# A token-major V stage, a shorter candidate list and other gather rates in a one-core hybrid decoder step

## The chip, the cores and the metric

The kernel runs on one core of one Trainium2 chip (trn2). The metric is the device time of one execution in microseconds. Three timed runs of the kernel before and one profiled execution are at hand.

## The reference, cut to what matters

The program computes one layer of a decoder for a prompt (16 meta tokens and 512 tokens) and 8 samples of 8 tokens: token mixers, then a product-key expert layer ("PEER"), then a final RMSNorm. The expert layer and the final norm are what the change touches:

```python
qh = einsum('td,de->te', xb, w_query)                  # 8 heads x 2 halves x 128
s  = einsum('thpd,hpnd->thpn', qh, sub_keys)           # 128 keys per half
sv, si = top_k(s, 16)                                  # best 16 keys of each half
cand = sv[:, :, 0, :, None] + sv[:, :, 1, None, :]     # 16 x 16 sums per head
top_s, pos = top_k(cand, 16)                           # best 16 pairs -> expert 128*i + j
gate = softmax(top_s)
act  = gelu(einsum('thkd,td->thk', expert_u[eidx], xb))
y    = einsum('thk,thkd->td', gate * act, expert_v[eidx])
h = h + y;  out = rms_norm(h, norm_final)              # 576 tokens of 1024
```

There are 16,384 experts, each a row of 1,024 numbers in `peer_u` and one in `peer_v`.

## The kernel before

All arithmetic is in fp32. A product is three fp32r matmuls (`mm3`, lines 135 to 139): each operand is split into a high part (written by ScalarE) and a low part (what is left, written by VectorE), and high times high, high times low and low times high are summed in PSUM.

Of the 576 tokens the first 384 (`ND`) are handled densely and the last 192 (`NG`) by gathers. **Dense** means that the hidden value of every expert is computed for every token. The experts are taken 128 at a time, a "half"; two halves make a pair, and there are 64 pairs (`NP`) and so 128 halves in the **U stage** (`hidden`, from line 1439) and as many in the **V stage** (`experts`, from line 1528). In the U stage a half's weights (128 x 1024) come by DMA seven halves ahead (`fetch`), ScalarE writes their high part three halves ahead (`hi`, line 1432), VectorE their low part two ahead (`lo`, line 1438), and 24 matmuls of 384 columns give the hidden values, which ScalarE passes through Gelu (line 1471) and which go to DRAM for the first 48 pairs (`gz`). In the V stage `prepare` reads them back, VectorE multiplies by the gates `wj` (line 1516), ScalarE and VectorE split the product into `ah` and `al` (lines 1518, 1523), and the 24 matmuls of a half have the weights' 128 x 128 pieces as the stationary operand and 384 columns of `ah` or `al` as the moving one, so that eight PSUM banks `py[d]` hold the output with its features on the partitions.

The **gates** come from the selection. `select` forms candidate sums of a head's best 16 and 16 keys, finds the best 16 of them with `top16` (`max`, `max_index`, `match_replace` on VectorE), and turns ranks back into key numbers. `taken`, `spread`, `onehots`, `scaled`, `scatter` and `stored` turn them, for the dense tokens, into a gate for every expert in DRAM (`wd`). `select(0)` belongs to the first block of gathered tokens and runs within `scored`, beside the scores of the other tokens; the other four blocks' selections are interleaved with the U stage by `route`.

The **gathered** tokens' experts come by indirect DMA, 128 rows of 4 KB at a time, 192 times from `peer_u` and 192 times from `peer_v` (`NROW` is 384; `gather_begin` on GpSimd's queue, `gather` on VectorE at lines 1344 and 1351). How many per half is a planner's matter: `gcred` grows by `GQ0` in each of the U stage's first 96 halves, by `GQ1` in its last 32, by `GQ2` in the V stage's first 32, and then by `rate`, which is worked out so that all are done `GTAIL` pairs before the end. `fill` spends VectorE's time of a half (`HALF` less `WL` and `MUL`) on gathers first and then on the steps of `route`; the numbers after `yield` are its costs in us. From `hidden` on, the order of PE, VectorE, ScalarE and SP is fixed as the program emits it (`in_order`). GpSimd's isn't, and what stands before `hidden` is ordered by the scheduler.

At the end of `experts` the last pair's matmuls run by `d`; VectorE adds the residual, ScalarE squares, PE sums over the partitions, the root is broadcast by PE, and eight transfers of 192 KB go out on SP's and ScalarE's queues (line 1598). The gathered tokens' own norm and output are `gather_out`.

Of the kernel before, what the change touches and what calls it, by code (L numbers as in the profile page):

```python
# [22 lines left out]
P = 128  # L23
# [7 lines left out]
H = 4  # L31
# [25 lines left out]
NCAND = 8 * TOPK + 8  # L57
# [9 lines left out]
GQ0, GQ1, GQ2, GTAIL = 1.25, 2.1, 1.65, 6  # L67
# [53 lines left out]
class Net:  # L121
# [108 lines left out]
    def build(self):  # L230
        tc, nc, I, O = self.tc, self.nc, self.I, self.O
        self.right = ExitStack()
        with self.pool("const") as cp, self.pool("wraw", 3) as self.wraw, self.pool("whl", 2) as self.whl, \
# [5 lines left out]
            self.yd = self.dp.tile([P, KC, ND], F32, name="yd")  # L239
# [5 lines left out]
            with self.pool("y") as yp:  # L245
# [688 lines left out]
    def merge(self):  # L934
# [3 lines left out]
        with self.pool("mg") as mp, self.pool("mw", 2) as wp, \  # L938
# [34 lines left out]
            for k in range(KC):  # L973
                nc.sync.dma_start(self.yd[:, k, :], self.y[k][:, :ND])
# [11 lines left out]
    def ffn_sink(self, o, w, ps, wp):  # L986
# [5 lines left out]
        def sink(k, t):  # L992
# [36 lines left out]
    def scored(self):  # L1029
# [4 lines left out]
        self.blks = [(NT - P, P), (ND, NX)] + TBLK  # L1034
# [13 lines left out]
        self.ijg = rp.tile([P, 3, ND], F16, name="ijg")  # L1048
        self.glo = rp.tile([P, ND], F32, name="glo")
# [3 lines left out]
        with self.pool("keys", 1, side="right") as kp, self.pool("qw", 2, side="right") as wp:  # L1053
            keys = kp.tile([P, 2 * PH, NK], F32, name="keys")
            nc.sync.dma_start(keys, I["keys"])
            for o, w in SEG:
# [52 lines left out]
                if o + w == NT:  # L1109
# [4 lines left out]
                    for d, v in ((self.x2h, self.xg[0]), (self.x2l, self.xg[1])):  # L1114
                        for k in range(KC):
                            nc.sync.dma_start(d[k][:, o:].bitcast(F32), v[k][:, :ND - o].bitcast(F32))

    def select(self, b):

# [24 lines left out]
        nc.vector.tensor_scalar(au[:n], ti[:n], 4, None, op0=ALU.logical_shift_right)  # L1144
        nc.vector.tensor_scalar(bu[:n], ti[:n], 15, None, op0=ALU.bitwise_and)
# [3 lines left out]
        nc.vector.scalar_tensor_tensor(t[:n], a[:n], 8.0, r[:n], op0=ALU.is_ge, op1=ALU.mult)  # L1149
        nc.vector.tensor_add(a[:n], a[:n], t[:n])  # L1150
        nc.vector.tensor_sub(r[:n], r[:n], t[:n])
        yield 0.9 + f
        out = []
        for x, rank in enumerate((a, r)):
            sb = small(f"sb{x}")
            nc.vector.tensor_copy(sb[:n], si[:n, b, :H, x, :])
# [19 lines left out]
        nc.vector.tensor_tensor(g[:n], g[:n], sm[:n, :, None].to_broadcast([n, H, TOPK]), op=ALU.mult)  # L1176
# [22 lines left out]
    def taken(self, b):  # L1199
# [12 lines left out]
        yield 1.3  # L1212
# [474 lines left out]
```

## Time and profile before

| | us |
|---|---|
| median of 3 runs | 1967.29 (1966.35 to 1970.87) |
| profiled execution, its own time | 1970.01 |
| its span in the profile | 1968.2 |
| PE busy | 1895.1 (96%) |
| VectorE busy | 1609.1 (82%) |
| ScalarE busy | 912.8 (46%) |
| GpSimd busy | 741.8 (38%) |
| mean granted TensorE clock | 0.982 of full speed |
| DMA, mean over the span | 279 GB/s |

The span runs from the first to the last instruction of the profiled execution; the time beside it is that execution's own. Matmul ends are modelled and matmuls overlap, so a busy PE says only that it had no gap.

### The profile page before, as it was taken

What the parts mean: (1) busy time and instruction counts of PE and PEld (TensorE: products, weight loads), DVE (VectorE), ACT (ScalarE), POOL (GpSimd) and SP (SyncE); (2) the same over time, 40 slices, a digit from 0 to 9 for tenths busy, and PEclk for the clock granted to TensorE, in tenths of its full rate; (3) what the DMA queues carried; (4) which work ended last, traced back from release to release, by engine and by line L of the source; (5) the groups of instructions that cost most, each with busy time, mean ns of one, the idle gap of its engine ahead of it and who ended that gap; (6) DMA issues with size and microseconds to landing.
All of it is one profiled execution on the core that took longest, in us unless ns stands there. A gap on an engine that the chain in (4) does not pass through costs nothing.

```text
span 1968.2 us, 33353 instructions
## 1 busy us (share of the span) xinstructions
PE 1895.1 (96%) x12481; PEld 1829.2 (93%) x12481; DVE 1609.1 (82%) x3016; ACT 912.8 (46%) x1594; POOL 741.8 (38%) x537
## 2 busy tenths in 40 slices
PE   8999999999999998999999999999999999999997
PEld 6898999788999997999999999999999999999996
DVE  6676676686366689999999998688999879889895
ACT  5542334263225454445777999533333323333332
POOL 1110010310001366243343444466776556656530
PEclk9998999999999998999999999999999999999998
DMA  7344233466455635799898999999999999999991
GB/s 264 111 152 140 92 104 103 149 184 197 159 164 164 200 125 168 265 328 325 340 358 322 394 396 368 384 390 395 400 400 400 399 401 400 399 402 400 401 340 57
DMA packets 219904, 548.20 MB, mean 279 GB/s; under 512 B 31332, under 2 KB 96612, under 8 KB 218076
## 3 DMA queue, kind: packets, MB, share of 16 engines
q1 hardware_dynamic: 163724, 343.90, 49.4%
q0 software_dynamic: 55296, 201.35, 26.5%
q8 instruction: 98, 1.61, 0.3%
q10 hardware_dynamic: 720, 0.80, 0.1%
q14 instruction: 66, 0.54, 0.1%
HBM read 474.89 MB, written 69.77 MB: 277 GB/s over the span
## 4 chain that ended last, share of the span: by engine, by line
PE 35%; DMA 19%; DVE 5%; issue 1%; POOL 0%; ACT 0%; SPq 0%; POOLq 0%; DVEq 0%; ACTq 0%
DMA wr<-in_v 9%; PE pz L137 8%; PE pz L139 8%; PE pz L138 8%; DMA wj<-wd 8%; PE py L138 2%; PE py L139 2%; PE py L137 2%; PE pw L1262 2%; DMA gz<-gz 2%; DVE ul L1438 1%; DVE gr L1344 1%; DMA yr<-yd 1%; DVE yt L1351 1%; DVE al L1523 0%
## 5 line engine op out<-in xcount | busy, mean ns | idle before, releaser
L1332 POOL DMA_INDIRECT gr<-in_ur,gi x192 | 308.5, 1607 | 272.9 <-DVE yt L1351 193.3
L1432 ACT ACTIVATE uh<-wr 128x1024 fp32r<-128x1024 f32 x256 | 270.5, 1057 | 250.2 <-PE py L138 123.8
L1332 POOL DMA_INDIRECT gr<-in_v,gi x192 | 289.4, 1507 | 238.0 <-DVE gr L1344 175.7
L138 PE MATMUL py<-al,uh 128*128 128x384 f32 x1024 | 349.2, 341 | 17.4 <-DVE al L1523 17.1
L137 PE MATMUL py<-ah,uh 128*128 128x384 f32 x1024 | 347.7, 340 | 4.0 <-ACT ah L1518 3.4
L137 PE MATMUL pz<-x2h,uh 128*128 128x384 f32 x1024 | 347.6, 339 | 0.0
L139 PE MATMUL py<-ah,ul 128*128 128x384 f32 x1024 | 347.5, 339 | 0.0
L139 PE MATMUL pz<-x2h,ul 128*128 128x384 f32 x1024 | 343.6, 336 | 2.0 <-DVE ul L1438 2.0
L138 PE MATMUL pz<-x2l,uh 128*128 128x384 f32 x1024 | 343.4, 335 | 0.0
L1438 DVE TENSOR_TENSOR ul<-wr,uh 128x1024 fp32r<-128x1024 f32 x256 | 311.9, 1218 | 15.6 <-issue 6.8
L1351 DVE SCALAR_TENSOR_TENSOR yt<-gr,ga,yt 128x1024 f32<-128x1024 f32 x192 | 245.8, 1280 | 15.0 <-DMA gr<-in_v,gi 12.5
L137 PE MATMUL acc<-xnh,wh 128*128 128x296 f32 (+1 forms) x768 | 233.7, 305 | 8.0 <-ACT xnh L296 6.3
L1344 DVE SCALAR_TENSOR_TENSOR gr<-gr,xt 128x1024 f32<-128x1024 f32 x192 | 233.5, 1217 | 6.4 <-DMA gr<-in_ur,gi 6.2
L139 PE MATMUL acc<-xnh,wl 128*128 128x296 f32 (+1 forms) x768 | 234.5, 306 | 0.5 <-DVE wl L133 0.5
L138 PE MATMUL acc<-xnl,wh 128*128 128x296 f32 (+1 forms) x768 | 233.9, 305 | 0.5 <-DVE xnl L297 0.5
L132 ACT ACTIVATE wh<-wr 128x1024 fp32r<-128x1024 f32 x104 | 110.0, 1059 | 226.7 <-PE acc L138 71.9
L138 PEld LDWEIGHTS py<-al,uh 128*128 128x128 f32 x1024 | 194.5, 190 | 21.3 <-DVE al L1523 21.2
L137 PEld LDWEIGHTS py<-ah,uh 128*128 128x128 f32 x1024 | 194.3, 190 | 5.3 <-ACT ah L1518 4.3
L139 PEld LDWEIGHTS pz<-x2h,ul 128*128 128x128 f32 x1024 | 193.0, 188 | 2.7 <-DVE ul L1438 2.6
L139 PEld LDWEIGHTS py<-ah,ul 128*128 128x128 f32 x1024 | 194.4, 190 | 0.0
L138 PEld LDWEIGHTS pz<-x2l,uh 128*128 128x128 f32 x1024 | 193.3, 189 | 0.0
L137 PEld LDWEIGHTS pz<-x2h,uh 128*128 128x128 f32 x1024 | 193.1, 189 | 0.1
(427 smaller groups left out, 3436.7 us busy)
## 6 DMA issues: line engine op xcount, KB each, us to landing
wr<-in_u SPq DMA_DIRECT2D x128, 512.0 KB
wr<-in_v SPq DMA_DIRECT2D x128, 512.0 KB
gz<-gz SPq DMA_DIRECT2D x96, 384.0 KB
wr<-in_w_in SPq DMA_DIRECT2D x48, 512.0 KB
wd<-wst SPq DMA_DIRECT2D x12, 2048.0 KB
wj<-wd SPq DMA_DIRECT2D x96, 256.0 KB
wr<-in_w_q SPq DMA_DIRECT2D x32, 512.0 KB
wr<-in_w_out SPq DMA_DIRECT2D x16, 512.0 KB
```

Of the source, the lines that this page charges most:

```text
L132: self.last_hi = self.nc.scalar.activation(hi, src, AF.Copy)
L137: mm(out, wh, xh, start=start, stop=False)
L138: mm(out, wh, xl, start=False, stop=False)
L139: self.last_mm = mm(out, wl, xh, start=False, stop=stop)
L1262: nc.tensor.matmul(pw[:, u, :], oh[0][:, t], oh[2 + x][:, t], start=x == 0, stop=x == 1)
L1332: nc.gpsimd.indirect_dma_start(out=t, out_offset=None, in_=src, in_offset=bass.IndirectOffsetOnAxis(ap=self.gi[z][:, x, c:c + 1], axis=0))
L1344: nc.vector.scalar_tensor_tensor(t, t, 1.0, xt, op0=ALU.mult, op1=ALU.mult, accum_out=ga[:, c:c + 1])
L1351: nc.vector.scalar_tensor_tensor(yt, t, ga[:, c:c + 1], yt, op0=ALU.mult, op1=ALU.add)
L1432: self.nc.scalar.activation(w, self.raws[s], AF.Copy)
L1438: self.nc.vector.tensor_sub(w, self.raws.pop(s), self.ws[s][0].bitcast(F32))
```

## The change

The V stage is turned round: the stationary operand is now 128 tokens of `ah` or `al`, the moving one 512 columns of the weights, so a half is 18 matmuls of 512 columns, and six PSUM banks hold the output with its tokens on the partitions. All products of a half with the weights' high part and `ah` come first, then the low part with `ah`, then the high part with `al`. The residual is added by PE: 24 fp32 matmuls with an identity, three in each of eight halves. The last pair runs by block of 128 tokens, and each block is normed over its free axis and sent out on its own. The first block's output goes in transfers of 112 and 15 rows, by two column halves; its first token goes out alone through the old feature-major output. The new `ND` is 1 and `NG` 575 for the host's outputs; `MD` is the old 384.

The candidate sums are 80 for each head (16 + 7 x 8 + 8) instead of 136, with three more small steps to turn a position into ranks. The two key-number copies become one, the last step of each sum tree writes the result itself, the gate's scaling moves into `select`, the copies of `taken` go to ScalarE, and two of the comparisons of `onehots` become one of twice the size. `GQ0` is 1.32 instead of 1.25, `GTAIL` 4 instead of 6. The other changes of the diff are the new names.

```diff
-NG = P + NX
-ND = NT - NG
+MG = P + NX
+MD = NT - MG
+ND, NG = 1, NT - 1
-NCAND = 8 * TOPK + 8
+NCAND = TOPK + 7 * 8 + 8
-GQ0, GQ1, GQ2, GTAIL = 1.25, 2.1, 1.65, 6
+GQ0, GQ1, GQ2, GTAIL = 1.32, 2.1, 1.65, 4
...
     def select(self, b):
-        nc.vector.tensor_tensor(cd[:n, :, :P].rearrange("p h (a b) -> p h a b", a=8),
-                                s0[:, :, :8, None].to_broadcast([n, H, 8, TOPK]),
-                                s1[:, :, None, :].to_broadcast([n, H, 8, TOPK]), op=ALU.add)
-        nc.vector.tensor_tensor(cd[:n, :, P:], s0[:, :, 8:], s1[:, :, 0:1].to_broadcast([n, H, 8]), op=ALU.add)
-        yield 0.2 + 1.15 * f
+        nc.vector.tensor_tensor(cd[:n, :, :TOPK], s0[:, :, 0:1].to_broadcast([n, H, TOPK]), s1, op=ALU.add)
+        nc.vector.tensor_tensor(cd[:n, :, TOPK:-8].rearrange("p h (a b) -> p h a b", b=8),
+                                s0[:, :, 1:8, None].to_broadcast([n, H, 7, 8]),
+                                s1[:, :, None, :8].to_broadcast([n, H, 7, 8]), op=ALU.add)
+        nc.vector.tensor_tensor(cd[:n, :, -8:], s0[:, :, 8:], s1[:, :, 0:1].to_broadcast([n, H, 8]), op=ALU.add)
+        yield 0.4 + 0.7 * f
...
-            yield 2.4
+            yield 1.93
...
+        w = small("rw")
+        nc.vector.tensor_scalar(w[:n], a[:n], 1.0, 8.0, op0=ALU.is_equal, op1=ALU.mult)
+        nc.vector.tensor_add(r[:n], r[:n], w[:n])
+        nc.vector.tensor_scalar(a[:n], a[:n], -1.0, 0.0, op0=ALU.add, op1=ALU.max)
...
+        sbs = wp.tile([P, H, 2, TOPK], BF, name="sb", tag="sb")
+        nc.vector.tensor_copy(sbs[:n], si[:n, b, :H])
...
-            v = small(f"ix{x}")
-            nc.vector.tensor_copy(v[:n], e[:n, :, 0, :])
...
     def taken(self, b):
-            nc.vector.tensor_copy(self.ijg[:, x, sl], p[:, :n])
-        gs = self.wp.tile([P, P], F32, name="gs", tag="gs")
-        nc.vector.tensor_scalar(gs[:, :n], g[:, :n], GSC, None, op0=ALU.mult)
-        nc.vector.tensor_copy(self.ijg[:, 2, sl], gs[:, :n])
-        nc.vector.tensor_sub(self.glo[:, sl], gs[:, :n], self.ijg[:, 2, sl])
+            nc.scalar.activation(self.ijg[:, x, sl], p[:, :n], AF.Copy)
+        nc.vector.tensor_copy(self.ijg[:, 2, sl], g[:, :n])
+        nc.vector.tensor_sub(self.glo[:, sl], g[:, :n], self.ijg[:, 2, sl])
...
     def onehots(self, q, last):
-        nc.vector.tensor_tensor(oh[1], io, rb(1), op=ALU.is_equal)
-        yield 0.61
-        nc.vector.tensor_tensor(oh[0], io, rb(0), op=ALU.is_equal)
-        yield 0.61
+        nc.vector.tensor_tensor(ij, io, r[:, :2].rearrange("p x t e -> p (x t) e")[:, :, None, :].to_broadcast([P, 2 * TG, N8, E8]),
+                                op=ALU.is_equal)
+        yield 1.15
...
     def experts(self):
+            def products(b, a, w, start=False, stop=False):
+
+                for c in range(2):
+                    nc.tensor.matmul(py[b][:, c, :], a[:, b * P:(b + 1) * P], w[:, 4 * c:4 * c + 4, :], start=start, stop=stop)
...
-                        for d in range(KC):
-                            self.mm3(py[d][:, :ND], wh[:, d, :], wl[:, d, :], ah[:, h], al[:, h], self.half == NK, False)
+                        for b in range(nb):
+                            products(b, ah[:, h], wh, start=s == NK)
+                        for b in range(nb):
+                            products(b, ah[:, h], wl)
+                        for b in range(nb):
+                            products(b, al[:, h], wh)
+                    d = s - NK - KEEP - 8
+                    if 0 <= d < KC:
+
+                        for b in range(nb):
+                            nc.tensor.matmul(py[b][:, d // 4, d % 4 * P:(d % 4 + 1) * P], self.y[d][:, b * P:(b + 1) * P], self.c("ident"),
+                                             start=False, stop=False)
...
+            for b in range(nb):
                 for h in range(2):
...
+                    wh, wl = self.ws[last - 1 + h]
+                    products(b, ah[:, h], wh)
+                    products(b, ah[:, h], wl)
+                    products(b, al[:, h], wh, stop=h == 1)
+                o = wp.tile([P, D], F32, name="yo", tag="yo", bufs=nb)
+                v = wp.tile([P, 1], F32, name="yv", tag="yv", bufs=nb)
+                nc.scalar.activation(o, py[b].rearrange("p a b -> p (a b)"), AF.Square, accum_out=v)
+                nc.vector.tensor_scalar(v, v, 1.0 / D, EPS, op0=ALU.mult, op1=ALU.add)
+                self.rsqrt(v, wp, bufs=2)
+                for c in range(2):
+                    sl = slice(c * 512, (c + 1) * 512)
+                    nc.vector.scalar_tensor_tensor(o[:, sl], py[b][:, c, :], v, self.gf[:, sl], op0=ALU.mult, op1=ALU.mult)
+                    if b:
+                        (nc.scalar if c else nc.sync).dma_start(self.O["yg"][b * P - ND:(b + 1) * P - ND, sl], o[:, sl])
+                    else:
+
+                        for n0, n1 in ((16, P), (ND, 16)):
+                            nc.sync.dma_start(self.O["yg"][n0 - ND:n1 - ND, sl], o[n0:n1, sl])
+                if b == 0:
+                    first = o
+
             for k in range(KC):
...
+                nc.tensor.matmul(one[:, k:k + 1], first[:ND, k * P:(k + 1) * P], self.c("ones")[:1, :1], start=True, stop=True,
+                                 skip_group_check=True)
+            v = wp.tile([P, KC], F32, name="y1")
+            nc.scalar.activation(v, one, AF.Copy)
+            nc.sync.dma_start(self.O["y"].rearrange("p k a -> p (k a)"), v)
```

## Rows read from the trace of the kernel before

**Rows 1.** The page, the span in 40 slices: DMA rate in GB/s.

```profile
GB/s 264 111 152 140 92 104 103 149 184 197 159 164 164 200 125 168 265 328 325 340 358 322 394 396 368 384 390 395 400 400 400 399 401 400 399 402 400 401 340 57
```

**Rows 2.** Windows by stage: length, busy us per engine, clock, DMA share, GB/s.

```profile
918.00:1250.00 332.00, 331.96 (x2416) 323.89 (x2415) 309.20 (x509) 279.53 (x670) 136.28 (x89) 1.00 0.94 361
1384.00:1517.50 133.50, 133.38 (x768) 133.12 (x769) 132.57 (x151) 46.54 (x50) 96.38 (x56) 1.00 1.03 400
1517.50:1900.20 382.70, 362.03 (x2017) 357.29 (x2016) 337.92 (x380) 124.70 (x130) 230.89 (x139) 0.98 1.03 400
1900.20:1942.10 41.90, 41.90 (x244) 41.90 (x243) 29.61 (x41) 15.14 (x17) 0.00 (x0) 1.00 0.43 142
```

**Rows 3.** The page, the chain that ended last, by line.

```profile
DMA wr<-in_v 9%; PE pz L137 8%; PE pz L139 8%; PE pz L138 8%; DMA wj<-wd 8%; PE py L138 2%; PE py L139 2%; PE py L137 2%; PE pw L1262 2%; DMA gz<-gz 2%; DVE ul L1438 1%; DVE gr L1344 1%; DMA yr<-yd 1%; DVE yt L1351 1%; DVE al L1523 0%
```

**Rows 4.** The page, costliest groups: busy us, mean ns, idle before.

```profile
L138 PE MATMUL py<-al,uh 128*128 128x384 f32 x1024 | 349.2, 341 | 17.4 <-DVE al L1523 17.1
L1351 DVE SCALAR_TENSOR_TENSOR yt<-gr,ga,yt 128x1024 f32<-128x1024 f32 x192 | 245.8, 1280 | 15.0 <-DMA gr<-in_v,gi 12.5
```

**Rows 5.** Windows of line 1332 alone, the indirect gathers issued on GpSimd.

```profile
1384.00:1517.50 133.50, 96.38 (x56) 1.00 1.03 400
1517.50:1900.20 382.70, 230.89 (x139) 0.98 1.03 400
```

**Rows 6.** PE's timeline (start us, us): matmuls of 256 and 384 columns.

```profile
764.93 0.28 PE L1091 MATMUL pq<-x2h,wh 128*128 128x256 f32 x1
...
767.32 0.28 PE L1091 MATMUL pq<-x2h,wh 128*128 128x256 f32 x1
...
1919.69 0.34 PE L137 MATMUL py<-ah,uh 128*128 128x384 f32 x1
...
1934.77 0.34 PE L137 MATMUL py<-ah,uh 128*128 128x384 f32 x1
```

**Rows 7.** The chain in order of time: four plain fp32 matmuls of 128 columns.

```profile
782.87 0.44 PE psc L1067 x4
```

**Rows 8.** Groups by form: search and fp32 matmul, ScalarE and VectorE on long rows.

```profile
L1021 DVE FIND_INDEX8 si<-sv,sc 128x8 uint32<-128x128 f32 x64 | 18.1, 282 | 0.0
L1021 DVE FIND_INDEX8 ti<-tv,cand 128x8 uint32<-128x136 f32 x36 | 10.1, 292 | 0.0
L772 PE MATMUL pss<-vm,ke 64*128 64x512 f32 x16 | 7.9, 615 | 1.4 <-DVE vm L764 1.4
L307 ACT ACTIVATE xt<-xt 128x1024 f32<-128x1024 f32 x4 | 4.2, 1060 | 1.6 <-DMA xt<-in_x 1.5
L794 DVE SCALAR_TENSOR_TENSOR at<-pkq,decay 128x512 f32<-128x512 f32 x4 | 2.7, 687 | 0.0
```

**Rows 9.** Timeline around the end of `select(0)`: VectorE, GpSimd (twice), PE.

```profile
765.57 0.47 DVE L1181 SCALAR_TENSOR_TENSOR gi<-ix,ix 128x128 int32<-128x128 bf16 x2
...
766.12 1.15 POOL L1332 DMA_INDIRECT gr<-in_ur,gi  x1 [2.98 <-DVE gi L1181]
...
771.03 4.68 POOL L133 TENSOR_TENSOR wl<-wr,wh 128x1024 fp32r<-128x1024 f32 x2
...
773.43 2.08 PE L1094 MATMUL pq<-x2h,wl 128*128 128x256 f32 x8 [5.72 <-POOL wl L133]
```

**Rows 10.** Timeline of the end: PE, VectorE (two), SP's queue.

```profile
1950.20 0.34 PE L139 MATMUL py<-ah,ul 128*128 128x384 f32 x1
...
1953.18 0.16 DVE L214 TENSOR_SCALAR rmsr<-py 128x3 f32<-128x3 f32 x1 [1.59 <-PE py L1586]
...
1954.42 0.16 DVE L163 TENSOR_TENSOR rmsr<-rsq,rst 128x3 f32<-128x3 f32 x1
...
1957.49 4.53 SPq L1598 DMA_DIRECT2D out_y<-yo  x4
```

**Rows 11.** Window after the last transfer's data: as in rows 2.

```profile
1964.00:1965.00 1.00, 0.00 (x0) 0.00 (x0) 0.00 (x0) 0.00 (x0) 0.00 (x0) 0.50 0.00 0
```

More of the change, by code (lines that the diff above doesn't have):

```diff
@@ L250, in build @@
                 with self.pool("x2") as xp:
-                    self.x2h = [xp.tile([P, ND], F32R, name=f"x2h{k}") for k in range(KC)]
-                    self.x2l = [xp.tile([P, ND], F32R, name=f"x2l{k}") for k in range(KC)]
+                    self.x2h = [xp.tile([P, MD], F32R, name=f"x2h{k}") for k in range(KC)]
+                    self.x2l = [xp.tile([P, MD], F32R, name=f"x2l{k}") for k in range(KC)]
                     with self.pool("x2g") as gp:
@@ L997, in sink @@
                 self.split(self.xg[0][k], self.xg[1][k], t)
-                for x, (dst, v, a) in enumerate(((self.xt, t, w - NG), (self.yt, self.y[k], ND))):
+                for x, (dst, v, a) in enumerate(((self.xt, t, w - MG), (self.yt, self.y[k], MD))):
                     if k % 2 == 0:
@@ L1165, in select @@
             w = TOPK
+            v = small(f"ix{x}")
             while w > 1:
                 w //= 2
-                nc.vector.tensor_add(e[:n, :, :w, :], e[:n, :, :w, :], e[:n, :, w:2 * w, :])
-                yield (w * H * TOPK) * 0.53e-3 + 0.1
-            v = small(f"ix{x}")
-            nc.vector.tensor_copy(v[:n], e[:n, :, 0, :])
+                nc.vector.tensor_add(e[:n, :, :w, :] if w > 1 else v[:n, :, None, :], e[:n, :, :w, :], e[:n, :, w:2 * w, :])
+                yield (w * H * TOPK) * 0.53e-3 + 0.15
             out.append(v.rearrange("p h k -> p (h k)"))
@@ L1443, in hidden @@
         tc, nc, I = self.tc, self.nc, self.I
-        self.wd = self.dp.tile([ND // TB, P, NK, TB], F32, name="wd")
-        self.gz = [self.dp.tile([P, 2, ND], F32, name=f"gz{j}") for j in range(NP - KEEP // 2)]
+        self.wd = self.dp.tile([MD // TB, P, NK, TB], F32, name="wd")
+        self.gz = [self.dp.tile([P, 2, MD], F32, name=f"gz{j}") for j in range(NP - KEEP // 2)]
         self.gdone, self.gcred, self.gready = 0, 0.0, True
@@ L1532, in experts @@
         self.run_due()
+        nb, last = MD // P, 2 * NK - 1
         with ExitStack() as es:
             yps = es.enter_context(self.pool("ey", 1, space=PSUM))
-            py = [yps.tile([P, 512], F32, name=f"py{d}") for d in range(KC)]
-            py = py[4:] + py[:4]
+            one = yps.tile([P, 2, 512], F32, name="one")[:, 0, :KC]
+            py = [yps.tile([P, 2, 512], F32, name=f"py{b}") for b in range(nb)]
+            py = py[1:] + py[:1]
             rate = (NROW - self.gdone - KEEP * GQ2) / (2 * (NP - GTAIL) - KEEP)
+            def products(b, a, w, start=False, stop=False):
+                for c in range(2):
+                    nc.tensor.matmul(py[b][:, c, :], a[:, b * P:(b + 1) * P], w[:, 4 * c:4 * c + 4, :], start=start, stop=stop)
             for k in range(NP, 2 * NP):
@@ L1556, in experts @@
                         self.gready, self.routing = False, self.gather_out()
-                    self.lo(self.half + 2)
-                    self.gates(self.half - NK + JG + 3)
+                    self.lo(s + 2)
+                    self.gates(s - NK + JG + 3)
                 if k == NP + KEEP // 2 - 1:
@@ L1562, in experts @@
                     self.gf = wp.tile([P, D], F32, name="gf")
-                    self.y = [wp.tile([P, ND], F32, name=f"yr{k}") for k in range(KC)]
+                    self.y = [wp.tile([P, MD], F32, name=f"yr{k}") for k in range(KC)]
                     nc.sync.dma_start(self.gf, I["gain"].to_broadcast([P, D]))
@@ L1568, in experts @@
                 pass
-            nb = (ND + P - 1) // P
-            sq = [wp.tile([P, ND], F32, name="rmssum" if d == 0 else "rmssq", tag="rmssum" if d == 0 else "rmssq", bufs=1 if d == 0 else 3)
-                  for d in range(KC)]
-            for d in range(KC):
+            for b in range(nb):
                 for h in range(2):
-                    w = self.ws[2 * NK - 2 + h]
-                    self.mm3(py[d][:, :ND], w[0][:, d, :], w[1][:, d, :], ah[:, h], al[:, h], False, h == 1)
-                nc.vector.tensor_add(self.y[d], self.y[d], py[d][:, :ND])
-                if 1 < d:
-                    nc.vector.tensor_add(sq[0], sq[0], sq[d - 1])
-                nc.scalar.activation(sq[d], self.y[d], AF.Square)
@@ L1582, in experts @@
-            col, t = py[0][:, :nb], py[1][:, :ND]
-            w = [min(P, ND - b * P) for b in range(nb)]
-            for b in range(nb):
-                for x in (0, KC - 1):
-                    nc.tensor.matmul(col[:w[b], b:b + 1], sq[x][:, b * P:b * P + w[b]], self.c("ones")[:, :1], start=x == 0, stop=x > 0)
-            rs = self.rms_cols(col, t, w, wp)
-            rb = wp.tile([P, ND], F32, name="rb")
-            nc.scalar.activation(rb, rs, AF.Copy)
-            for k in range(KC):
-                g = self.p("norm_final")[:, k:k + 1]
-                o = wp.tile([P, ND], F32, name="yo", bufs=KC)
-                if k in (2, 6):
-                    nc.scalar.activation(o, self.y[k], AF.Copy, scale=g)
-                    nc.gpsimd.tensor_mul(o, o, rb)
-                else:
-                    nc.vector.scalar_tensor_tensor(o, self.y[k], g, rs, op0=ALU.mult, op1=ALU.mult)
-                (nc.scalar if k % 2 else nc.sync).dma_start(self.O["y"][:, k, :], o)
+                    wh, wl = self.ws[last - 1 + h]
```

71 lines of the change are left out of this document (35 added, 36 removed).

## The prediction

> **What bounds the kernel now.** I read the slices first, then the windows by stage, the chain and the waits. The slices show DMA near 400 GB/s from slice 29 to slice 38 and below that nearly everywhere else [rows 1]. The windows say what limits each stage. In the middle of the U stage PE is busy 331.96 of 332 us and DMA runs at 361 GB/s: PE sets the pace. In the V stage's first 32 halves (133.5 us, 4.17 us a half) PE, VectorE (132.57) and DMA (400 GB/s) are all full. From there to the last gather, 382.7 us, DMA stays at 400 GB/s while PE idles 20.7 us and VectorE 44.8: DMA sets the pace. In the 41.9 us after it PE is full and DMA falls to 142 GB/s [rows 2]. The chain agrees: transfers of weights and gates hold the most of it beside the U stage's matmuls [rows 3]. PE's one large V wait, 17.1 us for `al` [rows 4], sits inside that DMA-bound stretch, so it is a symptom: taking it away lets PE reach the next late transfer sooner and no more.
>
> **What DMA has to move.** The planner's credits give 96 x 1.25 + 32 x 2.1 = 187 gathers in the U stage, 32 x 1.65 = 53 in the V stage's first 32 halves, and 144 in the next 84 halves (116 = 2 x 58 less 32). The trace has 56 and 139 issues there, with the rest a few issues ahead [rows 5]. A gather is 128 x 4 KB, 0.524 MB. A half also needs 0.524 MB of weights, 0.197 of `gz` and 0.197 of `wj` by the tiles' shapes. For 84 halves that is 77.1 MB, with 144 gathers 152.6 MB; 400 GB/s over 382.7 us is 153.1 MB [rows 2]. So the stretch is its bytes at 400 GB/s.
>
> **The gather rates.** `GQ0` at 1.32 moves 96 x 0.07 = 6.7 gathers, 3.5 MB, into the U stage. `GTAIL` at 4 lets the rest end at half 120, not 116, so four halves that ran at PE's pace with an idle DMA now share the load: their weights and `gz`, 4 x 0.721 = 2.9 MB, fall inside the stretch. It must move 153.1 - 3.5 + 2.9 = 152.5 MB, 381.2 us at 400 GB/s, and reaches half 120. Six halves are left before the last pair, where ten were. Their price is PE's.
>
> **PE's price of a half.** From start to start, 20 matmuls of 256 columns take 2.39 us, 119.5 ns each, and 87 of 384 columns 15.08 us, 173.3 ns each [rows 6]. The line through both gives 227.2 ns at 512: 18 of them are 4.09 us against 24 x 173.3 = 4.16. No row has an fp32r matmul of 512 columns, nor one with token data as the stationary operand. The bounds are 213 ns (columns at 2.4 GHz, nothing added) and 440: four plain fp32 matmuls of 128 columns take 0.44 us [rows 7], and 512 columns at that rate as much; one of 512 lasts 615 ns from its start to its end [rows 8]. I take 227, since it is the same kind of matmul.
>
> The Trainium skill (TensorE: Matmul & The Clock Gate, Back-to-back issue gap) gives columns / 2.4 + 2.5 ns, 162.5 at 384; the row shows 173.3, so it doesn't hold for this form here. By it a half would be 3.88 us and my sum 1.6 us less.
>
> Ten halves at 4.19 were 41.9 us [rows 2]; six at 4.09 are 24.5. From half 32 to the last pair: 382.7 + 41.9 = 424.6 before, 381.2 + 24.5 = 405.7 now, **-18.9 us**. Bounds: only the moved bytes, -8.8; or PE alone, 94 x 4.09 + 3.6 = 388.1, -36.5. The 3.6 is the identity matmuls: 24 x 0.11 = 2.6 [rows 7], and 1 us that I put on for changing between the two kinds. They come in halves 40 to 47, at 4.33 us a half by DMA, where PE then needs 4.54; the lag of 8 x 0.21 = 1.7 us at most is made up from the 0.24 us a half that PE has over in the 73 that follow, so nothing is added. They wait for `yr`, and the whole PE queue stands behind them, but those loads are issued eight halves, some 34 us, ahead. In the first 32 halves PE would give 32 x 0.07 = 2.2 us, but VectorE and DMA are as full; I take 0, with 2.2 as the other end.
>
> **The U stage.** 6.7 more gathers cost VectorE 6.7 x 1.28 = 8.6 us [rows 4] and DMA 3.5 MB over some 440 us, 8 GB/s on 361. VectorE is free for 22.8 us in the middle window [rows 2], and it gets back about 2.8 us for each of 3.5 selections (next part), the merged comparisons and `taken`. So nothing is added, and since PE is full nothing is won. The copies of `taken` wait on ScalarE for PE's transposes, with the next `hi` behind them; `hi` runs three halves ahead. If the cover were gone: +8.6.
>
> **The front.** PE waits 5.72 us for a low part from GpSimd, which stands behind four gathers, which wait for `select(0)`'s last step [rows 9]. A search over 128 columns takes 282 ns, over 136 292 [rows 8]: 10 ns for 8 columns, 70 for the 56 that go, and `select(0)` has 8 heads x 5 searches, 2.8 us. The shorter sums and the copies that go pay for the three new steps within some 0.3 us. GpSimd was free for 2.98 us before its first gather, so it can start as much earlier: **-2.8 us**. Bounds: 0, if the scheduler puts something else there, and -5.7, if the gap closes.
>
> **The end.** The last pair is 36 x 0.227 = 8.17 us after 48 x 0.173 = 8.32: **-0.15**. From PE's last matmul, 1950.20 + 0.34, to the end of the span are 17.7 us [rows 10]. Now each block needs a square (1.06 us, rows 8 has the like from SBUF), the root's small steps (1953.18 to 1954.58, 1.40 us, rows 10) and two products of 512 columns (0.69 each, rows 8): 3.8 us, after 2.7 us of PE. With T as PE's end, block 0 is done at T - 1.6 and block 1, whose small steps stand behind it on VectorE, at T + 1.2. Block 1's second transfer is issued by ScalarE and waits there for that product, and block 2's square stands behind it: T + 1.5 to T + 2.6. Its products end at T + 5.3, the copy of the first token and its transfer on SP at T + 6.2. The old last issue ended at 1962.02, 6.2 us before the span's end [rows 10]; so T + 12.4, **-5.3 us**. Bounds: -8 (no queueing on ScalarE, and with the data gone before 1964 [rows 11] only some 4.7 us after the last issue), and -3.
>
> **The sum.** -18.9 - 2.8 - 0.15 - 5.3 = -27.2. The profiled execution took 1970.0 us, its span 1968.2 with 1.8 around it; it becomes 1942.8. The runs' median is 2.7 below the profiled execution, so the median is forecast at 1940.
>
> **Rivals.** (a) *The later end of the gathers buys nothing.* After the last gather come `gather_out`'s steps, and with six halves instead of ten they, or the DMA's prefetch of the last weights, could hold the last pair; then only the 3.5 MB count, 8.8 us, and the time is 1950. For it: those steps have 17 us less; against it: 24.5 us are left, and VectorE was free for 12.3 of the 41.9 us [rows 2]. (b) *The U stage can't take the gathers*, VectorE becomes the bound there, +8.6: 1949. For it: its windows are nearly full; against: the 22.8 us. (c) *400 GB/s is not a ceiling but what was asked for*, and the V stage runs at PE's 388.1 us: 1923. Against it, PE idled 20.7 us at that rate and ten slices lie at 399 to 402 [rows 1]. The Trainium skill (DMA: Bandwidth & Descriptors, Specifications) has a fabric ceiling of 435 GB/s, and the trace stays under it. (d) *Slower: the wide fp32r matmul doesn't hold the line.* Nothing is felt up to 4.33 / 18 = 241 ns, as DMA hides it; all that is won is lost at (405.7 + 27.2) / 94 / 18 = 256 ns, and 260 ns give 1974 and more. For it: no such row; against: one line through both widths, and the weight loads get longer cover. That the change doesn't do what it says I hold for excluded where it counts bytes and columns.
>
> **Chances and range.** Forecast (1934 to 1946) 0.62; (a) 0.14; (b) 0.10; (c) 0.06; (d) 0.05, of which 0.04 is slower than before; the rest spread between. A difference under 0.2% (4 us) can't be told from none here. Faster 0.94, same 0.02, slower 0.04. The range takes in (a) and (b) and the bounds of front and end: 1929 to 1953.
>
> **What would show it.** Right: V windows at 400 GB/s to half 120, about 7 fewer gathers left when the V stage starts, matmuls 227 ns apart, a gap before the scores' low part of some 3 us, about 12 us from PE's last product to the end. Wrong: PE full in the V stage's later part, or waits of PE in the U stage, or matmuls above 241 ns.

## The result, and the profile after

The changed kernel takes 1940.03 us (median of 4 runs, 1938.06 to 1944.29); the kernel before, run beside it, 1966.82 (1966.28 to 1970.87). The ratio is 0.9862, 95% interval 0.984 to 0.9885: 26.8 us faster, as forecast (1940, -27.2). The steps behind that number did not all hold. The profiled execution took 1941.62 us, span 1939.4.

The page's slices answer to [rows 1]:

```profile
GB/s 267 103 158 156 87 112 100 140 190 181 175 166 149 211 130 158 248 343 332 348 354 344 398 396 380 376 401 397 402 400 401 397 399 402 400 398 401 399 401 103
```

The windows by stage answer to [rows 2], same columns: the middle of the U stage, V's first 32 halves, from there to the last gather, and from there to the last pair:

```profile
914.40:1246.40 332.00, 331.92 (x2404) 323.94 (x2403) 307.33 (x449) 278.39 (x669) 151.15 (x94) 1.00 0.97 368
...
1377.30:1511.90 134.60, 134.60 (x577) 108.31 (x578) 132.02 (x153) 46.49 (x50) 93.09 (x56) 1.00 1.04 401
1511.90:1897.70 385.80, 380.18 (x1648) 304.35 (x1647) 337.20 (x376) 129.65 (x137) 222.47 (x133) 1.00 1.03 397
1897.70:1921.10 23.40, 22.13 (x95) 17.54 (x94) 20.96 (x33) 8.09 (x10) 0.00 (x0) 1.00 0.23 75
```

DMA is at 397 to 401 GB/s there, as before. What has changed is the end: 23.4 us after the last gather instead of 41.9. 133 gathers are issued in the long stretch where there were 139 [rows 5]. PE, idle for 20.7 us there before, is idle for 5.6. The chain of waits in order of time (start, us, what), pieces of the V stage:

```profile
1377.29 172.46 PE py L1546 x738
1549.76 0.67 PE py L1564 x6
1550.42 4.20 PE py L1546 x18
...
1584.49 120.41 PE py L1546 x516
...
1709.20 7.90 DMA wr<-in_v
...
1875.09 15.87 DMA wj<-wd
```

By this chain PE sets the pace up to 1705 us; from 1709 to 1891 us transfers make up some 150 of the 182 us. A product of 512 columns takes 172.46 / 738 = 233.7 ns and a half 4.20 us, more than the old form's 4.16. The eight identity steps take 0.67 us each. PE's V groups on the page no longer wait for `al` (17.1 us in [rows 4]); 4.8 us are left for `ul` and 2.0 for `ah`:

```profile
L1546 PE MATMUL py<-ul,ah 128*128 128x512 f32 x768 | 201.3, 396 | 4.8 <-DVE ul L1440 4.8
L1546 PE MATMUL py<-uh,ah 128*128 128x512 f32 x768 | 201.6, 396 | 2.6 <-ACT ah L1520 2.0
```

The bytes of the long stretch, from the DMA view of 1511.9 to 1897.7 us (its rate in 40 slices, and the total):

```profile
GB/s 394 388 401 399 399 402 402 395 400 402 401 400 399 404 395 400 402 403 398 399 403 389 397 400 406 397 401 401 403 396 401 403 392 399 402 404 398 400 402 292
DMA packets 56956, 153.09 MB, mean 397 GB/s; under 512 B 5433, under 2 KB 22657, under 8 KB 56934
```

Profile against profile, in us:

| part | before | after | forecast | measured |
|---|---|---|---|---|
| start to the first scores' product (`pq`) | 653.0 | 649.1 | 0 | -3.9 |
| front, to the first `pz<-x2l` | 145.0 | 145.3 | -2.8 | +0.3 |
| U stage, to the first V product | 586.0 | 582.9 | 0 | -3.1 |
| V, first 32 halves | 133.5 | 134.6 | 0 | +1.1 |
| V, to the last gather | 382.7 | 385.8 | -1.5 | +3.1 |
| V, to the last pair | 41.9 | 23.4 | -17.4 | -18.5 |
| last pair | 8.4 | 8.6 | -0.15 | +0.2 |
| PE's end to the end of the span | 17.7 | 9.7 | -5.3 | -8.0 |

The first line is no gain. Up to that point both profiles have the same 4604 matmuls in the same order and 796 VectorE instructions, and the twelve kernels below, which are the same there, have their first `pq` between 645.9 and 655.6. From 130 to 260 us the granted clock was 0.93 in the profile before and in the latest of the twelve, 0.99 in the changed kernel's and in the earliest. The windows of 130 to 260 us, before and then after (the last three numbers are the clock, the DMA share and GB/s):

```profile
130.00:260.00 130.00, 126.52 (x941) 118.74 (x940) 91.09 (x152) 43.84 (x69) 9.48 (x27) 0.93 0.40 120
```

```profile
130.00:260.00 130.00, 125.72 (x979) 118.70 (x978) 96.69 (x168) 48.82 (x75) 9.49 (x27) 0.99 0.47 127
```

A median has this scatter in it too, so the experiments are read by stage.

### The profile page after: what moved, and what is told of

It is laid out like the page before. It is cut to its first block, busy times and chain, and to the rows that moved or that the text cites. A ratio compares the mean times of both kernels' runs of the same rounds, so it can differ in the third digit from the quotient of the medians.

```text
span 1939.4 us, 31893 instructions
## 1 busy us (share of the span) xinstructions
PE 1889.3 (97%) x11759; PEld 1722.4 (89%) x11759; DVE 1592.7 (82%) x2962; ACT 909.2 (47%) x1598; POOL 745.1 (38%) x535
## 4 chain that ended last, share of the span: by engine, by line
PE 78%; DMA 11%; DVE 9%; issue 1%; ACT 1%; SPq 0%; DVEq 0%; ACTq 0%
PE py L1546 18%; PE pz L138 9%; PE pz L140 9%; PE pz L139 9%; PE acc L138 4%; PE acc L140 4%; PE acc L139 4%; DMA wr<-in_v 4%; DMA wj<-wd 3%; PE pw L1264 2%; PE py L664 1%; PE pz L659 1%; PE pq L1095 1%; PE pq L1092 1%; PE pbr L138 1%
## 5 line engine op out<-in xcount | busy, mean ns | idle before, releaser
L1334 POOL DMA_INDIRECT gr<-in_ur,gi x192 | 302.8, 1577 | 265.1 <-DVE yt L1353 200.7
L1334 POOL DMA_INDIRECT gr<-in_v,gi x192 | 300.6, 1566 | 238.8 <-DVE gr L1346 177.3
L140 PE MATMUL acc<-xnh,wl 128*128 128x296 f32 (+1 forms) x768 | 233.3, 305 | 0.1
L1546 PE MATMUL py<-ul,ah 128*128 128x512 f32 x768 | 201.3, 396 | 4.8 <-DVE ul L1440 4.8
L1546 PE MATMUL py<-uh,ah 128*128 128x512 f32 x768 | 201.6, 396 | 2.6 <-ACT ah L1520 2.0
L1546 PE MATMUL py<-uh,al 128*128 128x512 f32 x768 | 200.5, 395 | 0.0
L1546 PEld LDWEIGHTS py<-ul,ah 128*128 128x128 f32 x768 | 143.5, 188 | 42.1 <-DVE ul L1440 7.8
L1546 PEld LDWEIGHTS py<-uh,ah 128*128 128x128 f32 x768 | 143.2, 188 | 38.2 <-ACT ah L1520 3.5
L1546 PEld LDWEIGHTS py<-uh,al 128*128 128x128 f32 x768 | 144.1, 188 | 35.1
```

What stands on the lines that cost most here:

```text
L140: self.last_mm = mm(out, wl, xh, start=False, stop=stop)
L1334: nc.gpsimd.indirect_dma_start(out=t, out_offset=None, in_=src, in_offset=bass.IndirectOffsetOnAxis(ap=self.gi[z][:, x, c:c + 1], axis=0))
L1546: nc.tensor.matmul(py[b][:, c, :], a[:, b * P:(b + 1) * P], w[:, 4 * c:4 * c + 4, :], start=start, stop=stop)
```

## Experiments

The stages of every kernel's profile, from the views by tile (`pq`, `pz`, `py`): front and U as above; V from its first product to the start of its last; the tail from there to the end of the span.

| kernel | front | U | V | tail | time (median) |
|---|---|---|---|---|---|
| before | 145.0 | 586.0 | 566.2 | 18.0 | 1966.8 |
| changed | 145.3 | 582.9 | 552.0 | 10.1 | 1940.0 |
| 1 changed, old rates | 143.2 | 583.1 | 561.9 | 10.1 | 1951.9 |
| 2 before, `GTAIL` 4 | 143.1 | 586.7 | 560.7 | 18.0 | 1958.7 |
| 3 before, both new rates | 142.2 | 593.9 | 552.9 | 17.3 | 1959.4 |
| 4 changed, old selection | 142.7 | 591.0 | 550.1 | 10.1 | 1946.1 |
| 5 changed, no identity | 142.4 | 584.0 | 551.4 | 10.0 | 1940.3 |
| 6 changed, 448 columns | 144.2 | 584.6 | 550.0 | 10.9 | 1943.4 |
| 7 changed, 384 columns | 143.7 | 585.7 | 549.1 | 11.3 | 1947.6 |
| 8 changed, one bank | 144.3 | 584.1 | 552.6 | 10.1 | 1940.2 |
| 9 changed, tail on SyncE | 144.2 | 583.9 | 549.8 | 7.7 | 1942.1 |
| 10 changed, 1.36 and 3 | 144.0 | 585.1 | 543.3 | 10.1 | 1933.0 |
| 11 edits of 9 and 10 | 142.7 | 583.6 | 544.5 | 7.7 | 1934.8 |
| 12 as 11, no identity | 142.7 | 585.3 | 545.8 | 7.7 | 1932.9 |

Numbers 6 to 8 are one run each. Every stage is read from one profile, and it scatters: the V stage, whose work number 9 leaves alone and number 8 leaves the same in size, has 549.8 and 552.6 where the changed kernel has 552.0, and the ten profiles with the new selection have fronts from 142.4 to 145.3. A difference of less than some 3 us in one stage shows nothing by itself.

**1. The rates undone.**

```diff
-GQ0, GQ1, GQ2, GTAIL = 1.32, 2.1, 1.65, 4
+GQ0, GQ1, GQ2, GTAIL = 1.25, 2.1, 1.65, 6
```

> The changed kernel with the old gather rates (GQ0 1.25, GTAIL 6); everything else as changed. Theory 1 (the V stage's gain comes from the bytes: gathers moved into the U stage and the later end of the gathers): the V stage takes back what the prediction gave to the rates, 14 to 19 us, and the time is 1954 to 1959 us; the last gather ends four halves earlier and PE idles more before it. Rival (the token-major products carry the gain, by ending the wait for al): at most 3 us slower, 1940 to 1943, with a V stage of about 544 us as in the changed kernel.

Measured: 1951.87 us, ratio to before 0.9922 (0.9908 to 0.9937). V takes back 9.9 us, below theory 1's 14 but far from the rival's 3, and the time is below theory 1's 1954 to 1959.

**2. Only the later end, in the kernel before.**

```diff
-GQ0, GQ1, GQ2, GTAIL = 1.25, 2.1, 1.65, 6
+GQ0, GQ1, GQ2, GTAIL = 1.25, 2.1, 1.65, 4
```

> The kernel before with GTAIL 4 in place of 6 and nothing else; the gathers of the U stage stay at 187. By the prediction's sum the stretch from half 32 to the last gather then moves 153.1 + 2.9 = 156.0 MB, 390.0 us at 400 GB/s, and six halves of 4.19 us (25.1) follow where ten did (41.9): 415.1 us against 424.6, so -9.5 us, about 1957 us. Rival (the later end of the gathers buys nothing, as their last steps or the wait for al hold the last pair): within 2 us of the kernel before, 1965 to 1969.

Measured: 1958.67 us, 0.996 (0.9947 to 0.9973), -8.1 us; V is 5.5 us shorter, where the sum had 9.5: after the last gather come 25.2 us, as forecast, but the stretch up to it took 394.0 us and not 390.0. The later end is worth something without token-major products, and rival (a) falls.

**3. Both rates in the kernel before.**

```diff
-GU, GV = 1.2, 1.22
-GQ0, GQ1, GQ2, GTAIL = 1.25, 2.1, 1.65, 6
+GU, GV = 1.1, 1.12
+GQ0, GQ1, GQ2, GTAIL = 1.32, 2.1, 1.65, 4
```

> The kernel before with both new rates (GQ0 1.32, GTAIL 4), its old feature-major products and its old selection; the planner's price of a gather is 1.1 and 1.12 us, not 1.2 and 1.22, so that its U stage plans the 6.7 further gathers beside the longer selections. Theory 1 (the bytes carry the V stage's gain): the V stage is 14 to 19 us shorter, the time 1948 to 1953. Rival A (the products' form and the wait for al carry it): 1965 to 1968. Rival B (without the cheaper selection VectorE can't take the gathers in the U stage): the U stage is up to 8.6 us longer, and of the 14 to 19 us 5 to 10 are left, 1957 to 1962, with waits of PE in the U stage.

Measured: 1959.38 us, 0.9966 (0.9954 to 0.9978). V is 13.3 us shorter in the old form, nearly all of the changed kernel's 14.2, so the bytes carry the V gain; the 0.9 us left for the products' form is within scatter. With number 2's 5.5 us for the later end, 7.8 are left for the moved gathers, whose bytes are 8.8 us by my sum. Rival B holds as well, and the time is in its range: the U stage is 7.9 us longer. By PE's groups from 790 to 1383.9 us it waits for VectorE's low parts and for a one-hot that ScalarE makes; in all PE is idle for 7.0 us there, against 0.7 in the changed kernel's U stage:

```profile
L139 PE MATMUL pz<-x2h,ul 128*128 128x384 f32 x1024 | 344.9, 337 | 4.0 <-DVE ul L1438 3.9
...
L1262 PE MATMUL pw<-oh,oh 128*128 128x128 f16 x768 | 52.6, 220 | 2.5 <-ACT oh L1247 2.3
```

**4. The old selection in the changed kernel** (candidates, decoding, `taken`).

```diff
-NCAND = TOPK + 7 * 8 + 8
-GU, GV = 1.2, 1.22
+NCAND = 8 * TOPK + 8
+GU, GV = 1.1, 1.12
...
-            nc.scalar.activation(self.ijg[:, x, sl], p[:, :n], AF.Copy)
+            nc.vector.tensor_copy(self.ijg[:, x, sl], p[:, :n])
```

> The changed kernel with the old selection from 136 candidates and its old hand-over to the one-hots; rates 1.32 and 4, the planner's price of a gather 1.1 and 1.12 us so that its plan fits. Theory 1 (the cheaper selection is what lets VectorE take the further gathers in the U stage, and it is worth nothing in the front): the U stage 6 to 9 us longer than the changed kernel's 583, the front unchanged within 1.5 us, the time 1946 to 1949. Rival A (as the prediction had it, it is worth 2.8 us in the front and nothing in the U stage, whose cover is enough): 1943. Rival B (it is worth both): 1949 to 1952.

Measured: 1946.14 us, 0.9894 (0.9875 to 0.9914): theory 1. U is 8.1 us longer; the front, 142.7, is not longer at all. In numbers 3 and 4 the planner's price of a gather was lowered so that the plan fits, so what they show is a U stage with that many gathers beside the old selection.

**5. Without the identity matmuls.**

```diff
-                        for b in range(nb):
-                            nc.tensor.matmul(py[b][:, d // 4, d % 4 * P:(d % 4 + 1) * P], self.y[d][:, b * P:(b + 1) * P], self.c("ident"),
-                                             start=False, stop=False)
```

> The changed kernel without the 24 identity matmuls (the residual is left out of the output). The trace of the changed kernel has eight halves of 4.87 us with them against 4.20, 5.3 us in all. Theory 1 (DMA sets the end of the V stage, as the prediction has it, and PE's time ahead of the late transfers is cover): the 5.3 us come back as waits for weights and gates before the last gather, and the time is within 1 us of the changed kernel, 1939 to 1940. Rival (PE sets the V stage throughout): 5.3 us less, 1934 to 1935.

Measured: 1940.33 us, V 0.6 us shorter, within scatter and far from the rival's 5.3: theory 1. By the groups of V, the wait for `ah` grew from 2.0 to 4.8 us:

```profile
L1546 PE MATMUL py<-uh,ah 128*128 128x512 f32 x757 | 198.2, 396 | 5.4 <-ACT ah L1520 4.8 <-ACT gk L1490 0.6
```

**6 to 8. The price of a 512-column product.** Number 6 cuts the V products to 448 columns:

```diff
+WC = 448
...
-                    nc.tensor.matmul(py[b][:, c, :], a[:, b * P:(b + 1) * P], w[:, 4 * c:4 * c + 4, :], start=start, stop=stop)
+                    wd = w.rearrange("p c e -> p (c e)")
+                    nc.tensor.matmul(py[b][:, c, :512 if start else WC], a[:, b * P:(b + 1) * P], wd[:, 512 * c:512 * c + (512 if start else WC)], start=start, stop=stop)
```

> The changed kernel with V products of 448 columns, not 512 (the first half's products keep 512; the last 64 columns of each 512 are left out of the sums). The step from start to start was 119.5 ns at 256 columns, 173.3 at 384 and 233.7 at 512. Theory 1 (one line to 384 and a dearer stretch from there): 203 to 204 ns. Theory 2 (the line through 256 and 384 holds to 448, and what costs more sets in only at the full 512): 200 ns. Theory 3 (a constant of 6.5 ns that this form pays at any width): 207 ns. The time: with PE at 3.6 to 3.7 us a half the early V stage is DMA's as well, so at most 8 us less than the changed kernel, 1932 to 1940.

Number 7 has `WC = 384`:

> The changed kernel with V products of 384 columns in each bank of 512 (the last 128 columns of each are left out of the sums, except in the first half). Steps from start to start so far: 119.5 ns at 256 and 173.3 at 384 in the U stage's form (weights stationary, one PSUM bank for the whole half), 205.4 at 448 and 233.7 at 512 in the V stage's new form (tokens stationary, another bank with every matmul). Theory 1 (the new form adds some 5 to 6 ns at any width): 178 to 180 ns. Theory 2 (the width does it, above 384): 173 to 174 ns. Read where PE runs without waits; the total says little, since DMA sets the pace.

Number 8 keeps 512 columns in one bank:

```diff
-                    nc.tensor.matmul(py[b][:, c, :], a[
+                    nc.tensor.matmul(py[b][:, c if start or stop else 0, :], a[
```

> The changed kernel with both 512-column products of a block going into the same PSUM bank between the first half and the last pair (the sums are of other columns then); stationary and moving operands as they were. Theory 1 (going to another bank with every matmul is what adds 6.5 ns): 227 to 230 ns from start to start. Theory 2 (the bank makes no difference): 233 to 234 ns.

PE's timeline (start, us of the group, matmuls in it) where it runs without waits, for 448 columns, then 384, then one bank:

```profile
1418.04 1.39 PE L1548 MATMUL py<-uh,al 128*128 128x448 f32 x6
...
1422.97 1.39 PE L1548 MATMUL py<-uh,ah 128*128 128x448 f32 x6
```

```profile
1446.77 1.22 PE L1548 MATMUL py<-uh,al 128*128 128x384 f32 x6
...
1449.96 0.34 PE L1548 MATMUL py<-uh,al 128*128 128x384 f32 x1
```

```profile
1415.90 1.56 PE L1546 MATMUL py<-uh,al 128*128 128x512 f32 x6
...
1424.30 1.10 PE L1546 MATMUL py<-uh,al 128*128 128x512 f32 x4
```

From start to start that is 4.93 / 24 = 205.4 ns, 3.19 / 18 = 177.2 and 8.40 / 36 = 233.3. Going to another bank costs nothing: theory 2 of number 8. At 448 columns 205.4 lies between theories 1 and 3 of number 6. At 384 columns this form takes 177.2 where the old products take 173.3 (read in the old V stage [rows 6]; the old U stage has the same from 1299.76 to 1304.96 us), so theory 1 of number 7 holds in kind, though with 4 ns and not 5 to 6. The three widths lie on one line of 0.44 ns a column; the old forms at 256 and 384 gave 0.42. Number 6's time, 1943.4 us, is above the 1932 to 1940 expected: V is only 2.0 us shorter.

The windows of number 7 in the V stage also answer rival (c), 400 GB/s as no ceiling:

```profile
1519.00:1700.00 181.00, 145.98 (x769) 138.19 (x768) 154.59 (x177) 57.92 (x63) 105.20 (x63) 0.92 1.04 400
1700.00:1800.00 100.00, 80.21 (x407) 74.62 (x406) 87.64 (x102) 33.13 (x35) 59.28 (x36) 0.94 1.03 400
```

PE is idle for a fifth of the time, VectorE, the fullest engine, for over a tenth, and DMA gives no more than 400. With a quarter of the products' columns gone, V is only 2.9 us shorter. The Trainium skill (DMA: Bandwidth & Descriptors, Specifications) puts the fabric's ceiling at 435 GB/s; no rate shown here is above 406.

**9. The output transfers on SyncE.**

```diff
-                        (nc.scalar if c else nc.sync).dma_start(self.O["yg"][b * P - ND:(b + 1) * P - ND, sl], o[:, sl])
+                        nc.sync.dma_start(self.O["yg"][b * P - ND:(b + 1) * P - ND, sl], o[:, sl])
```

> The changed kernel with every output transfer of blocks 1 and 2 issued by SyncE; ScalarE issues none. In the changed kernel's trace block 2's square starts 1.7 us after PE's last product, right behind the transfer that ScalarE issues for block 1 once its product is there. Theory (that transfer holds the square, the square holds the end): the square starts within 0.2 us of PE's last product, and from there to the end of the span are 8.0 us where 9.7 were; the time is 1.5 to 2.3 us less, 1937.7 to 1938.5. Rival (VectorE, which is at block 1's product until 1.3 us after PE's end, or SyncE's queue with four more transfers sets the end): the square starts earlier and the end stays where it was, within 0.7 us.

The timeline of the tail, first of the changed kernel, then of number 9:

```profile
1929.08 0.63 PE L1546 MATMUL py<-uh,al 128*128 128x512 f32 x2
...
1929.55 1.41 DVE L1603 SCALAR_TENSOR_TENSOR yo<-py,yv,gf 128x512 f32<-128x512 f32 x2
...
1931.04 0.35 ACTq L1605 DMA_DIRECT2D out_yg<-yo  x1
1931.43 1.02 ACT L1598 ACTIVATE yo<-py 128x1024 f32<-128x1024 f32 x1 [2.95 <-DVE yo L1603]
...
1936.12 0.33 SPq L1618 DMA_DIRECT2D out_y<-y  x1
```

```profile
1923.56 0.63 PE L1546 MATMUL py<-uh,al 128*128 128x512 f32 x2
...
1924.22 1.02 ACT L1598 ACTIVATE yo<-py 128x1024 f32<-128x1024 f32 x1 [1.27 <-PE py L1546]
...
1928.69 0.41 SPq L1618 DMA_DIRECT2D out_y<-y  x1
```

The square starts with PE's end, not 1.7 us after it, and the tail is 2.4 us shorter, more than the 1.7 expected; numbers 11 and 12 have the same 7.7. The medians don't show it: 1942.06 (1933.75 to 1943.93; 0.9863 to 0.9902) lies within the scatter of 1940.03.

**10. More gathers in U, the end two halves later.**

```diff
-GQ0, GQ1, GQ2, GTAIL = 1.32, 2.1, 1.65, 4
+GQ0, GQ1, GQ2, GTAIL = 1.36, 2.1, 1.65, 3
```

> The changed kernel with GQ0 1.36 and GTAIL 3: 3.8 further gathers (2.0 MB) in the U stage, and the gathers may end two halves later. Bytes alone: 5.0 us at 400 GB/s, and two halves that cost 1.8 us of DMA each in place of 4.2 us of PE, 4.8 us: the V stage 8 to 10 us shorter, no more, since PE needs 535 of its 544 us. Theory 1 (VectorE's cover in the U stage is used up by 1.32, as the kernel before with the new rates had a U stage 7.9 us longer): the U stage 3 to 5 us longer, the time 4 to 6 us less, 1934 to 1936. Rival A (cover is left): the U stage as it is, 1930 to 1932. Rival B (the steps after the last gather hold the last pair with so few halves left): the V stage at most 3 us shorter, 1937 to 1943.

Measured: 1933.02 us, 0.9837 (0.9821 to 0.9854). V is 8.7 us shorter, as the bytes say, and U 2.2 us longer, below theory 1's 3 to 5. With the same rates number 11 has 583.6 and number 12 585.3, while the kernels with 1.32 and the new selection lie between 582.9 and 585.7, so what U pays can't be told from scatter. In the windows of V, its first 32 halves and from there to 1901, PE has no idle time left:

```profile
1383.30:1517.90 134.60, 134.59 (x577) 108.31 (x578) 132.93 (x154) 46.46 (x50) 94.29 (x56) 1.00 1.03 401
1517.90:1901.00 383.10, 383.10 (x1669) 309.14 (x1668) 336.94 (x375) 131.49 (x139) 213.45 (x129) 1.00 1.03 398
```

**11. Both edits.** The diffs of 9 and 10 together.

> The changed kernel with GQ0 1.36 and GTAIL 3 and with the output transfers of blocks 1 and 2 on SyncE: the two edits that shortened a stage in their traces. Theory: the two add up, the V stage stays PE's (543 us to its last product where the changed kernel has 552) and the tail is 7.7 us where it has 10.1; with a U stage up to 2 us longer the time is 1930 to 1933, 34 to 37 us less than the kernel before. Rival (the gain of the tail is lost, as the one run's median said: 1942): 1933 to 1936.

Measured: 1934.76 us, 0.9844 (0.9829 to 0.9859). Each stage is as the theory has it (V 544.5 for 543, within scatter); the median is the rival's. From the first `pq` to the end of the span it takes 1278.5 us, against 1290.3 changed and 1315.2 before: the shortest with the full output.

**12. Number 11 without the identity matmuls**, with number 5's diff.

> The kernel of the run before without its identity matmuls (the residual is left out of the output). With the slower rates, where DMA set the end of the V stage, leaving them out was worth nothing. Theory (now PE is full for the whole V stage): its 5.3 us come out, the V stage to its last product goes from 543 to 538 us. Rival (DMA takes over at once, at 398 GB/s it is at its limit too): at most 2 us, 541 to 543.

Measured: 1932.92 us, V 545.8 against 544.5. The theory fell: PE was full, and 5.3 us less of its work bought nothing. PE then waited 3.5 us for `ah` and 1.2 for `ul`, where number 11 has none for `ah` and 0.6 for `ul`. By the groups of V:

```profile
L1546 PE MATMUL py<-uh,ah 128*128 128x512 f32 x760 | 198.4, 396 | 4.2 <-ACT ah L1520 3.5 <-ACT gk L1490 0.6
```

At these rates the two limits lie on top of each other.

## Why the total was right, by the prediction's steps

**V as bytes (-18.9 from half 32 on; measured -15.4, and -14.3 with the first 32 halves).** The mechanism was right: the last gather ends at half 120, and the old form with both rates has nearly the same gain. Three sizes were off. The stretch to the last gather took 385.8 us, not 381.2: it moved 153.1 MB, not 152.5 (1.5 us), at a mean of 397 GB/s (3.1 us), because the rate doesn't end square; the last of its 40 slices has 292. The first 32 halves cost 1.1 us where I had 0, at 4.20 a half. And the last pair started 5.6 halves after the last gather, not 6 at 4.09, which gave 1.1 back. The wait for `al` was mostly a symptom: with the old rates and the new form (number 1) its 17.1 us are gone, 9.0 us for `ah` stand there, and V gains 4.3:

```profile
L1546 PE MATMUL py<-uh,ah 128*128 128x512 f32 x757 | 201.0, 401 | 9.6 <-ACT ah L1520 9.0 <-ACT gk L1490 0.6
```

A sign that I had named for being wrong came in part: PE is full up to 1705 us, in a stretch that I gave to DMA alone. PE's own need from half 32 to the last pair, 94 x 4.20 + 5.3 = 400.1 us, is only 9 us less than the 409.2 it took; my bound had 388.1.

**PE's price of a half (4.09; measured 4.20).** This step failed: the line through 256 and 384 columns came from another form and was 6.5 ns short at 512; by number 7, 4 ns of that is the form and the rest its steeper line. The claim that nothing is felt up to 241 ns nearly held, as DMA hid all but the first 32 halves. The Trainium skill (TensorE: Matmul & The Clock Gate, Back-to-back issue gap) gives 215.8 ns at 512 columns by the rule that I cited, which it calls the gap of an isolated matmul; for a stream of loads and matmuls it has about 131 ns. The trace's 233.7 is above both.

**Identity matmuls (3.6 us, hidden).** They took 8 x 0.67 = 5.3 us and were hidden (number 5). My reading of [rows 7] was wrong: the trace records each plain fp32 matmul of 128 columns as two (the three identity matmuls of a step are x6 in the chain), so its four records are two matmuls of 0.22 us, and 24 x 0.22 is the 5.3. The 1 us for changing between the two kinds of matmul is shown by no run, and nothing is left for it.

**U stage (0; measured -3.1).** My claim that the selection's time pays for the gathers is what numbers 3 and 4 show from the other side: without it U is 7.9 and 8.1 us longer, where I had +8.6 for a lost cover. The 3 us on top do not come from the rates, as number 1 has the same U; PE's idle time fell from 2.5 to 0.7 us. The seven kernels with the new selection and 1.25 or 1.32 have a mean of 584.0, the two before with the old rates 586.0 and 586.7, so some 2 us of it may be more than scatter; the two sets nearly touch (585.7 and 586.0).

**Front (-2.8; measured +0.3).** The step "it can start as much earlier" held in part, and the conclusion failed. It is not the scatter of one profile: the four kernels with the old selection have a mean of 143.3, the ten with the new one 143.7. Counted from the first `pq`, GpSimd's first gather starts at 111.3 us where it started at 113.1 [rows 9], 1.8 earlier and not 2.8. The timeline of GpSimd and PE:

```profile
760.43 1.15 POOL L1334 DMA_INDIRECT gr<-in_ur,gi  x1 [2.69 <-DVE gi L1189]
...
767.75 2.08 PE L1095 MATMUL pq<-x2h,wl 128*128 128x256 f32 x8 [5.31 <-POOL wl L134]
```

PE's wait ends 1.8 us earlier as well, at 118.7 from the first `pq` where it was 120.4. But it now stands ahead of more work (148 `pq` matmuls follow it to the U stage where 120 did) and is as long, 5.31 against 5.72. The rest went to an earlier wait. PE's score products (`psc`) wait for `qT`, a copy that stands behind steps of `select(0)` on ScalarE. That wait ends 95.6 us after the first `pq` in both profiles, but in the new order, which before `hidden` is the scheduler's, PE comes to it 3.4 us sooner, with 24 fewer `pq` matmuls done. Before, then after:

```profile
748.64 1.22 PE L1067 MATMUL psc<-keys,qT 128*128 128x128 f32 x4 [2.71 <-ACT qT L1096]
```

```profile
744.75 1.22 PE L1068 MATMUL psc<-keys,qT 128*128 128x128 f32 x4 [6.12 <-ACT qT L1097]
```

The longest wait for `qT` is 6.1 us in all ten profiles with the new selection and 2.7 to 3.7 in the four with the old one. PE's groups from 700 to 800 us, before and then after:

```profile
L1094 PE MATMUL pq<-x2h,wl 128*128 128x256 f32 x128 | 19.6, 299 | 6.0 <-POOL wl L133 6.0
L1067 PE MATMUL psc<-keys,qT 128*128 128x128 f32 x93 | 16.0, 298 | 6.5 <-ACT qT L1096 6.4
```

```profile
L1095 PE MATMUL pq<-x2h,wl 128*128 128x256 f32 x128 | 19.3, 297 | 5.3 <-POOL wl L134 5.3
L1068 PE MATMUL psc<-keys,qT 128*128 128x128 f32 x91 | 15.6, 298 | 8.4 <-ACT qT L1097 8.3
```

The waits of these groups are 12.5 us before and 13.7 after. My bound of 0, if the scheduler puts something else there, is what came. I costed one wait and not the others on PE's way, and no run holds the order fixed.

**Tail (-5.3; measured -8.0).** The path was as described, ScalarE's queue holding block 2's square included (number 9). The last issue ended at T + 6.75, forecast T + 6.2; from there to the end of the span are 2.95 us, not the 6.2 that I took over from the old tail, whose last issue was one of four on SP [rows 10]. Why the end follows so much sooner was not tested.

So the total was right by luck: V and front, 7.7 us short together, were nearly made up by U and tail, 5.8 more than forecast, and with the last pair 24.9 us are left of the 27.2. From span to span the 3.9 us of the first stretch, where the clocks differ, come on top, 28.8 in all; the medians differ by 26.8. Of the signs named for being right, 400 GB/s to half 120 and some 7 fewer gathers in V (189 issues where there were 195 [rows 5]) came; 227 ns, a gap of some 3 us in the front and 12 us of tail did not. Of the rivals, (b)'s mechanism exists but needs the old selection; (a) and (c) fell (numbers 2 and 7); (d)'s premise came true, off the line, but below the 241 ns from which it was to be felt.

## What to carry to other kernels

Where a stage runs at a steady transfer rate, count its bytes and ask where else they can go: rates alone gave the old products nearly the whole V gain, but the stage that took the gathers gave 8 us back until another edit freed the engine that consumes the data there. A full PE doesn't say that taking PE work away pays: take some away and see whether the next limit stands right behind it. When a stage that nothing touched moves by 4 to 10 us between profiles, compare stage by stage before reading a median.

## What the runs showed of the hardware

Fp32r matmuls with token data stationary and weights moving step by 177.2, 205.4 and 233.3 to 233.7 ns at 384, 448 and 512 columns, 0.44 ns a column, at a granted clock of 1.00; with weights stationary the step is 173.3 ns at 384. The PSUM bank doesn't matter, and the cause stays open. A plain fp32 matmul of 128 columns is recorded as two and takes 0.22 us. DMA stayed at 400 GB/s whether PE was full or a fifth idle.
